# Feed-forward matmuls taken two by two: both products with the weights' high parts, then both with their low parts

## The chip, the cores and the metric

The kernel runs on one core of one Trainium2 chip. The metric is device time in microseconds (us) of one execution; shorter is better. Three executions of the kernel before gave 979.96, 982.59 and 986.15 us; their median is 982.59 us.

## The reference: what is computed

Two layers act on 256 tokens of width 1024. Each layer is a feed-forward block, a mixing block (two kinds of attention, a gated product over tokens, a pooling) and a second feed-forward block, each with a residual:

```python
def swiglu_ffn(x, g, w1, w3, w2):
    h = rms_norm(x, g)
    return (jax.nn.silu(h @ w1) * (h @ w3)) @ w2
...
        x = x + FFN_RES_WEIGHT * swiglu_ffn(x, ffn1_norm[l], ffn1_w1[l], ffn1_w3[l], ffn1_w2[l])
...
        x = x + FFN_RES_WEIGHT * swiglu_ffn(x, ffn2_norm[l], ffn2_w1[l], ffn2_w3[l], ffn2_w2[l])
```

`w1` and `w3` are 1024 x 2816, `w2` is 2816 x 1024, all in float32. So there are four feed-forward blocks in one execution; they are called block 1 to block 4 here.

## The kernel before

**Numbers in two parts.** Every float32 operand of a large product is split into a high part (`h`, or the first half of a tile `hl`), which ScalarE rounds to the type float32r, and a low part (`lo`, or the second half of `hl`), which VectorE gets as the difference (`split`, lines 122 and 123, for weights; `split_scaled` for activations). A product of two such operands is taken as high*high + high*low + low*high.

**The helper `mm2` (lines 149 and 150)** does one such product of a 128x128 block of weights with a 128x256 block of activations. Its first matmul has the weights' high part as the stationary operand and streams 512 columns past it: the activations' high part (256 columns) and low part (256 columns), which lie side by side in one tile. The results go to the two halves of one PSUM bank. Its second matmul has the weights' low part as the stationary operand, streams the 256 columns of the activations' high part, and adds to the first half of the same bank. Every matmul has a weight load of its own, so a product is load, 512 columns, load, 256 columns. The helper `mm3` (lines 143 to 145) serves the mixing block and is untouched; it takes three matmuls of equal width for a product.

**Up stage.** For each of the 22 blocks `m` of 128 hidden units, `up(m)` has one 1 MB tile of weights loaded and split, takes two banks (`j` = 0 for `w1`, 1 for `w3`), and for each of the 8 blocks `k` of the width calls `up_products(m, k)`, which calls `mm2` once for each `j`. That is 16 products for each `m`, 352 for a stage. `act(m)` then adds the halves of each bank (ScalarE line 303, VectorE line 304), applies the norm's factor, SiLU and the gate, and splits the result into `hid[m]` (lines 134 and 135). In block 1, `up_first` takes `m` = 0 and 1 together, piece by piece as their weights land. `rows` and `sums` put a few small matmuls (lines 224 and 243) among the products of `m` = 2 or so.

**Down stage.** `down(c)`, for 8 output blocks `c`, adds up 22 products (one for each `m`, one `mm2` each) in one bank: 176 products for a stage. `finish` adds the result to the residual `x` (line 234).

**What sets the order.** SyncE issues the weight loads, as far ahead as the four raw tiles allow; ScalarE and VectorE split them into four tiles for the two parts. The order on each engine's queue is fixed before the run by the framework's planner, which follows the order of the program but moves ahead of an instruction whose input it expects to be late another one whose inputs it expects to be there. In part of the mixing block the order written is pinned; in the feed-forward blocks it is not. Each engine runs its queue in order.

Of the kernel before, what the change touches and what calls it, by code (L numbers as in the profile page):

```python
# [29 lines left out]
T = 256  # L30
D = 1024
DFF = 2816
NM = DFF // 128
# [37 lines left out]
def tile_macaron(ctx, tc, xT, g0, const0, consts, params, w13, w2, wA, wB, wD, wC, wE, wcmp, wo, out):  # L71
    nc = tc.nc
# [14 lines left out]
    def bank_a():  # L87
        a = banks.tile([128, 512], F32, name="a", tag="bank")
        return a

    def bank_h():
        h = banks.tile([128, 512], F32, name="h", tag="bank")
        return h

    def s2():
        s = tiles.tile([128, 512], F32, name="s", tag="tile")
        return s

    def halves(s):
        return s.rearrange("p (a n) -> p a n", a=2)  # L100
# [11 lines left out]
    def split(src, n, cuts=2, loads=1):  # L112

        h = spl.tile([128, 2048], F32R)
        lo = spl.tile([128, 2048], F32R)
        r = raws.tile([128, 2048], F32)

        def part(a, b):
            nc.sync.dma_start(r[:, a:b], src[:, a:b])
            for i in range(a, b, n // cuts):  # L120
                c = slice(i, min(i + n // cuts, b))
                nc.scalar.activation(h[:, c], r[:, c], AF.Copy)  # L122
                nc.vector.tensor_tensor(lo[:, c], r[:, c], h[:, c].bitcast(F32), op=ALU.subtract)  # L123

        for i in range(loads):
            part(n * i // loads, n * (i + 1) // loads)
        return (h[:, :n], lo[:, :n]) if loads else (h[:, :n], lo[:, :n], part)

    def split_scaled(src, scale, n=T):

        hl = tiles.tile([128, 2 * n], F32R, name="hl", tag="tile")
        th, tl = hl[:, :n], hl[:, n:]
        if scale is None:
            nc.scalar.activation(th, src, AF.Copy)  # L134
            nc.vector.tensor_tensor(tl, src, th.bitcast(F32), op=ALU.subtract)  # L135
        else:
            nc.scalar.activation(th, src, AF.Copy, scale=scale)
            nc.vector.scalar_tensor_tensor(tl, src, scale, th.bitcast(F32), op0=ALU.mult, op1=ALU.subtract)  # L138
        return th, tl, hl
# [4 lines left out]
        nc.tensor.matmul(o, wgt[0], mov[1], start=False, stop=False)  # L144
        return nc.tensor.matmul(o, wgt[1], mov[0], start=False, stop=stop)  # L145

    def mm2(o, wgt, mov, start, stop):

        nc.tensor.matmul(o, wgt[0], mov[2], start=start, stop=False)  # L149
        return nc.tensor.matmul(o[:, :T], wgt[1], mov[0], start=False, stop=stop)  # L150

    g0t = const.tile([128, 8 * L], F32)
    x = const.tile([128, 8, T], F32)
# [77 lines left out]
    def finish(k, accs, factor, norm):  # L231

        for acc in accs:
            nc.vector.scalar_tensor_tensor(x[:, k, :], acc, factor, x[:, k, :], op0=ALU.mult, op1=ALU.add)  # L234
        if norm is not None:
            norm.chunk(k)
        else:
            nc.sync.dma_start(out[:, k, :], x[:, k, :])

    def bcast_rows(rstd):  # L240
        p = bank_h()
        for t in range(2):
            nc.tensor.transpose(p[:, 128 * t:128 * t + 128], rstd[:, t:t + 1].to_broadcast([128, 128]), ident)  # L243
        rb = wk.tile([128, T], F32)
        nc.vector.tensor_copy(rb, p[:, :T])
        return rb

    def ffn(l, f, norm, gain, at_step):

        first = norm is None  # L250
        if first:
            norm = Norm(g0t)
        w13s, hid, w2s, st = {}, {}, {}, {}

        def up_products(m, k):
            h, lo = w13s[m]
            for j in range(2):
                c = slice(256 * k + 128 * j, 256 * k + 128 * j + 128)
                ins = mm2(st[m][j], (h[:, c], lo[:, c]), norm.xs[k], k == 0, k == 7)
            return ins  # L260

        def up_first():

            parts = []
            for m in range(2):
                st[m] = [bank_h(), bank_h()]
                h, lo, part = split(w13[l, f, m], 2048, loads=0)
                w13s[m] = h, lo
                parts.append(part)
            for a, b in ((0, 1), (1, 2), (2, 4), (4, 6), (6, 8)):  # L270
                if a:
                    nc.sync.dma_start(x[:, a:b, :], xT[:, a:b, :])
                if not a:
                    norm.operand(0)
                for part in parts:
                    part(256 * a, 256 * b)
                for k in range(a, b):
                    if k:
                        norm.operand(k)
                for k in range(a, b):  # L280
                    for m in range(2):
                        up_products(m, k)
            for fn in at_step.get(1, ()):
                fn()
            for k in range(8):
                norm.square(k)
            norm.total()

        def up(m, mid={}):
            w13s[m] = split(w13[l, f, m], 2048, cuts=4 if m < 3 else 2, loads=2 if first and m == 2 else 1)  # L290
            for fn in at_step.get(m, ()):
                fn()
            st[m] = [bank_h(), bank_h()]
            for k in range(8):
                ins = up_products(m, k)
                if k in mid:
                    with tc.issue_after(ins.ins):
                        mid[k]()

        def act(m):  # L300
            hr = halves(s2())
            for j in range(2):
                nc.scalar.activation(hr[:, j, :], st[m][j][:, T:], AF.Copy)  # L303
                nc.vector.tensor_tensor(hr[:, j, :], st[m][j][:, :T], hr[:, j, :], op=ALU.add)  # L304
            nc.vector.tensor_tensor(hr, hr, st["rb"].unsqueeze(1).to_broadcast([128, 2, T]), op=ALU.mult)  # L305
            gt = hr[:, 0, :]
            nc.scalar.activation(gt, gt, AF.Silu)  # L307
            nc.vector.tensor_tensor(gt, gt, hr[:, 1, :], op=ALU.mult)  # L308
            hid[m] = split_scaled(gt, None)

        def w2_slot(i):
            w2s[i] = split(w2[l, f, i], 2048, cuts=2)

        def down(c):
            acc = bank_a()
            for m in range(NM):
                i, o = divmod(NM * c + m, 16)
                if i not in w2s:
                    w2_slot(i)
                s = slice(128 * o, 128 * o + 128)  # L320
                mm2(acc, (w2s[i][0][:, s], w2s[i][1][:, s]), hid[m], m == 0, m == NM - 1)
            return halves(acc)

        def sums():
            st["rstd"] = norm.rstd()

        def rows():
            st["rb"] = bcast_rows(st["rstd"])
            act(0)
            act(1)  # L330

        for m in range(NM):
            if not (first and m < 2):
                up(m, ({5: sums, 7: rows} if first else {3: rows}) if m == 2 else {})
            elif m == 0:
                up_first()
            if m == 1 and not first:
                norm.total()
                sums()
            if m > 1:  # L340
                act(m)
        nxt = None if gain is None else Norm(gain)
        for c in range(8):
            acc = down(c)
            finish(c, (acc[:, 0, :], acc[:, 1, :]), 0.5, nxt)
        return nxt
# [608 lines left out]
    norm = None  # L955
    for l in range(L):
# [5 lines left out]
        o, w = _PAR["mix_g"]  # L962
        norm = ffn(l, 0, norm, par[:, o:o + w], steps)
        norm = mixer(l, norm, par)
        norm = ffn(l, 1, norm, None if l == L - 1 else g0t[:, 8 * l + 8:8 * l + 16], {})
# [112 lines left out]
```

## Time and profile before

| | |
|---|---|
| median of three executions | 982.59 us |
| the profiled execution | 982.34 us |
| its span, first to last instruction | 980.5 us |
| TensorE matmul busy | 964.3 us (98%), 5840 matmuls |
| weight loads busy | 838.0 us (85%), 5840 loads |
| VectorE busy | 698.6 us (71%) |
| ScalarE busy | 530.6 us (54%) |
| mean granted TensorE clock | 0.996 of full speed |

Times are in us from the start of the span. PE is TensorE's matmuls, PEld its weight loads, which run beside the matmuls; DVE is VectorE, ACT ScalarE. L149 is line 149 of the kernel. The duration shown for a matmul reaches from its start to a modelled end, and successive matmuls overlap: two rows with 0.40 and 0.28 us start again after some 0.35 us. What a matmul costs TensorE in a dense stretch is therefore read from one start to the next start, not from its duration.

### The profile page before, as it was taken

What the parts mean: (1) busy time and instruction counts of PE and PEld (TensorE: products, weight loads), DVE (VectorE), ACT (ScalarE), POOL (GpSimd) and SP (SyncE); (2) the same over time, 40 slices, a digit from 0 to 9 for tenths busy, and PEclk for the clock granted to TensorE, in tenths of its full rate; (3) what the DMA queues carried; (4) which work ended last, traced back from release to release, by engine and by line L of the source; (5) the groups of instructions that cost most, each with busy time, mean ns of one, the idle gap of its engine ahead of it and who ended that gap; (6) DMA issues with size and microseconds to landing.
All of it is one profiled execution on the core that took longest, in us unless ns stands there. A gap on an engine that the chain in (4) does not pass through costs nothing. (4 is left out here: it accounts for less than half of the span.)

```text
span 980.5 us, 14915 instructions
## 1 busy us (share of the span) xinstructions
PE 964.3 (98%) x5840; PEld 838.0 (85%) x5840; DVE 698.6 (71%) x1256; ACT 530.6 (54%) x971; POOL 66.0 (7%) x67
## 2 busy tenths in 40 slices
PE   8999999999989999999999999999998999999998
PEld 6888888898869888888888888889987898888887
DVE  5987776575778777776667777755666787777751
ACT  7655555363566555655445655544545665555530
POOL 2000000031102000000010000001220030000000
PEclk9999999999999999999999999999999999999999
DMA  8965554445426655555555555545453455555530
GB/s 306 338 230 196 172 191 174 159 145 215 173 94 233 232 173 189 197 172 196 191 172 187 200 172 188 197 152 184 169 203 114 150 211 175 177 196 188 177 108 17
DMA packets 28150, 179.28 MB, mean 183 GB/s; under 512 B 3248, under 2 KB 5168, under 8 KB 8240
## 3 DMA queue, kind: packets, MB, share of 16 engines
q1 hardware_dynamic: 27792, 178.19, 52.1%
q8 instruction: 46, 0.75, 0.3%
q10 hardware_dynamic: 288, 0.14, 0.1%
q14 instruction: 24, 0.20, 0.1%
HBM read 177.27 MB, written 1.05 MB: 182 GB/s over the span
## 5 line engine op out<-in xcount | busy, mean ns | idle before, releaser
L123 DVE TENSOR_TENSOR lo<-r,h 128x1024 fp32r<-128x1024 f32 (+4 forms) x346 | 391.7, 1148 | 163.4 <-ACT h L122 162.7
L149 PE MATMUL h<-hl,h 128*128 128x512 f32 x1408 | 498.7, 399 | 1.4 <-ACT h L122 0.8
L122 ACT ACTIVATE h<-r 128x1024 fp32r<-128x1024 f32 (+4 forms) x346 | 327.8, 973 | 268.1 <-issue 230.6
L150 PE MATMUL h<-hl,lo 128*128 128x256 f32 x1408 | 395.3, 281 | 0.5 <-DVE lo L123 0.5
L149 PEld LDWEIGHTS h<-hl,h 128*128 128x128 f32 x1408 | 264.4, 188 | 67.9 <-DVE hl L138 1.5
L150 PEld LDWEIGHTS h<-hl,lo 128*128 128x128 f32 x1408 | 265.8, 189 | 2.1 <-DVE lo L123 2.1
L149 PE MATMUL a<-hl,h 128*128 128x512 f32 x704 | 246.9, 395 | 0.0
L150 PE MATMUL a<-hl,lo 128*128 128x256 f32 x704 | 197.3, 280 | 0.0
L149 PEld LDWEIGHTS a<-hl,h 128*128 128x128 f32 x704 | 131.9, 187 | 31.5 <-DVE hl L135 0.9
L150 PEld LDWEIGHTS a<-hl,lo 128*128 128x128 f32 x704 | 133.0, 189 | 0.0
L234 DVE SCALAR_TENSOR_TENSOR x<-a,x 128x256 f32<-128x256 f32 x80 | 32.9, 421 | 49.0 <-PE a L150 45.3
L304 DVE TENSOR_TENSOR s<-h,s 128x256 f32<-128x256 f32 x176 | 65.9, 415 | 1.1 <-ACT s L303 1.1
L305 DVE TENSOR_TENSOR s<-s,rb 128x512 f32<-128x512 f32 x88 | 60.9, 692 | 2.8
L134 ACT ACTIVATE hl<-s 128x256 fp32r<-128x256 f32 x92 | 38.2, 417 | 43.4 <-DVE s L308 33.9
L303 ACT ACTIVATE s<-h 128x256 f32<-128x256 f32 x176 | 56.5, 371 | 2.7 <-PE h L150 2.7
L211 POOL TENSOR_TENSOR s<-s 128x512 f32<-128x512 f32 x12 | 16.8, 1402 | 593.3 <-ACT s L207 593.3
L143 PE MATMUL a<-h,hl 128*128 128x384 f32 (+2 forms) x128 | 45.8, 358 | 0.0
L307 ACT ACTIVATE s<-s 128x256 f32<-128x256 f32 x88 | 35.5, 404 | 17.9 <-DVE s L305 17.8
L145 PE MATMUL a<-h,hl 128*128 128x384 f32 (+2 forms) x128 | 45.0, 351 | 0.0
L144 PE MATMUL a<-lo,hl 128*128 128x384 f32 (+2 forms) x128 | 44.9, 351 | 0.0
L135 DVE TENSOR_TENSOR hl<-s,hl 128x256 fp32r<-128x256 f32 x92 | 38.4, 419 | 3.4 <-ACT hl L134 3.4
L308 DVE TENSOR_TENSOR s<-s 128x256 f32<-128x256 f32 x88 | 36.8, 419 | 3.4 <-ACT s L307 3.4
(187 smaller groups left out, 779.1 us busy)
## 6 DMA issues: line engine op xcount, KB each, us to landing
r<-in_w_dram SPq DMA_DIRECT2D x129, 1024.0 KB, 4.8
r<-in_wcmp_dram SPq DMA_DIRECT2D x8, 1024.0 KB, 4.8
r<-in_wo_dram SPq DMA_DIRECT2D x8, 1024.0 KB, 5.4
r<-in_wE_dram SPq DMA_DIRECT2D x4, 1024.0 KB, 4.7
r<-in_wC_dram SPq DMA_DIRECT2D x4, 1024.0 KB, 4.7
r<-in_wD_dram SPq DMA_DIRECT2D x4, 800.0 KB, 4.3
r<-in_wA_dram SPq DMA_DIRECT2D x4, 768.0 KB, 4.4
r<-in_wB_dram SPq DMA_DIRECT2D x4, 768.0 KB, 4.3
```

Source lines behind the costliest of these rows:

```text
L122: nc.scalar.activation(h[:, c], r[:, c], AF.Copy)
L123: nc.vector.tensor_tensor(lo[:, c], r[:, c], h[:, c].bitcast(F32), op=ALU.subtract)
L134: nc.scalar.activation(th, src, AF.Copy)
L135: nc.vector.tensor_tensor(tl, src, th.bitcast(F32), op=ALU.subtract)
L143: nc.tensor.matmul(o, wgt[0], mov[0], start=start, stop=False)
L144: nc.tensor.matmul(o, wgt[0], mov[1], start=False, stop=False)
L145: return nc.tensor.matmul(o, wgt[1], mov[0], start=False, stop=stop)
L149: nc.tensor.matmul(o, wgt[0], mov[2], start=start, stop=False)
L150: return nc.tensor.matmul(o[:, :T], wgt[1], mov[0], start=False, stop=stop)
L303: nc.scalar.activation(hr[:, j, :], st[m][j][:, T:], AF.Copy)
L304: nc.vector.tensor_tensor(hr[:, j, :], st[m][j][:, :T], hr[:, j, :], op=ALU.add)
L305: nc.vector.tensor_tensor(hr, hr, st["rb"].unsqueeze(1).to_broadcast([128, 2, T]), op=ALU.mult)
```

## The change

`mm2` goes, and `mm2x2` takes its place. It is given two products and issues four matmuls: the 512 columns of the first product, the 512 columns of the second, the 256 columns of the first, the 256 columns of the second. In the up stage the two products are `j` = 0 and 1 of one `k`: they have the same activations and two different banks. In the down stage they are `m` and `m + 1` of one `c`, with different activations and the same bank. `NM` is 22 and a weight tile of the down stage holds 16 blocks, so both products of a pair always lie in one tile. The number of matmuls and of weight loads, their widths and the data that they read are as before, and so is everything outside `up_products` and `down`.

```diff
-    def mm2(o, wgt, mov, start, stop):
-
-        nc.tensor.matmul(o, wgt[0], mov[2], start=start, stop=False)
-        return nc.tensor.matmul(o[:, :T], wgt[1], mov[0], start=False, stop=stop)
+    def mm2x2(os, wgts, movs, starts, stops):
+
+
+        for o, wgt, mov, start in zip(os, wgts, movs, starts):
+            nc.tensor.matmul(o, wgt[0], mov[2], start=start, stop=False)
+        for o, wgt, mov, stop in zip(os, wgts, movs, stops):
+            ins = nc.tensor.matmul(o[:, :T], wgt[1], mov[0], start=False, stop=stop)
+        return ins
...
             h, lo = w13s[m]
-            for j in range(2):
-                c = slice(256 * k + 128 * j, 256 * k + 128 * j + 128)
-                ins = mm2(st[m][j], (h[:, c], lo[:, c]), norm.xs[k], k == 0, k == 7)
-            return ins
+            c = [slice(256 * k + 128 * j, 256 * k + 128 * j + 128) for j in range(2)]
+            return mm2x2(st[m], [(h[:, s], lo[:, s]) for s in c], (norm.xs[k],) * 2, (k == 0,) * 2, (k == 7,) * 2)
...
-            for m in range(NM):
+            for m in range(0, NM, 2):
                 i, o = divmod(NM * c + m, 16)
                 if i not in w2s:
                     w2_slot(i)
-                s = slice(128 * o, 128 * o + 128)
-                mm2(acc, (w2s[i][0][:, s], w2s[i][1][:, s]), hid[m], m == 0, m == NM - 1)
+                w = [(w2s[i][0][:, s], w2s[i][1][:, s]) for s in (slice(128 * o, 128 * o + 128),
+                                                                  slice(128 * o + 128, 128 * o + 256))]
+                mm2x2((acc, acc), w, (hid[m], hid[m + 1]), (m == 0, False), (False, m == NM - 2))
```

## Rows read from the trace of the kernel before

**Rows 1.** The page's first part: busy time, share of the span and instructions of each engine.

```profile
PE 964.3 (98%) x5840; PEld 838.0 (85%) x5840; DVE 698.6 (71%) x1256; ACT 530.6 (54%) x971; POOL 66.0 (7%) x67
```

**Rows 2.** The page's costliest groups, those of the two lines that the change touches: h is a bank of the up stage, a one of the down stage. Columns: count, busy us, mean ns of one, idle us of the engine just before them and what ended it.

```profile
L149 PE MATMUL h<-hl,h 128*128 128x512 f32 x1408 | 498.7, 399 | 1.4 <-ACT h L122 0.8
L150 PE MATMUL h<-hl,lo 128*128 128x256 f32 x1408 | 395.3, 281 | 0.5 <-DVE lo L123 0.5
...
L149 PE MATMUL a<-hl,h 128*128 128x512 f32 x704 | 246.9, 395 | 0.0
L150 PE MATMUL a<-hl,lo 128*128 128x256 f32 x704 | 197.3, 280 | 0.0
```

**Rows 3.** Two stretches of the table by windows, the load-paced beginning and a stretch in block 2: length, busy us (count) of PE, PEld, DVE, ACT and POOL, granted clock, mean busy share of the DMA engines, GB/s.

```profile
0.00:50.00 50.00, 46.58 (x240) 38.01 (x241) 38.27 (x62) 33.26 (x59) 7.95 (x13) 1.00 0.90 321
...
300.00:400.00 100.00, 100.00 (x587) 87.59 (x586) 79.04 (x127) 60.17 (x107) 7.93 (x5) 1.00 0.57 200
```

**Rows 4.** The timeline of PE in the up stage of block 2: start us, duration us, instruction. The last row is the start of the product 30 products after the first one.

```profile
330.30 0.40 PE L149 MATMUL h<-hl,h 128*128 128x512 f32 x1
330.54 0.28 PE L150 MATMUL h<-hl,lo 128*128 128x256 f32 x1
330.66 0.40 PE L149 MATMUL h<-hl,h 128*128 128x512 f32 x1
330.89 0.28 PE L150 MATMUL h<-hl,lo 128*128 128x256 f32 x1
331.01 0.40 PE L149 MATMUL h<-hl,h 128*128 128x512 f32 x1
...
340.90 0.40 PE L149 MATMUL h<-hl,h 128*128 128x512 f32 x1
```

**Rows 5.** The timeline of PE in the down stage of block 1; the last row again 30 products after the first.

```profile
160.25 0.39 PE L149 MATMUL a<-hl,h 128*128 128x512 f32 x1
160.48 0.28 PE L150 MATMUL a<-hl,lo 128*128 128x256 f32 x1
160.60 0.39 PE L149 MATMUL a<-hl,h 128*128 128x512 f32 x1
...
170.65 0.39 PE L149 MATMUL a<-hl,h 128*128 128x512 f32 x1
```

**Rows 6.** The timeline of PE in the mixing block of layer 1, where `mm3` issues only matmuls of 256 columns, all into one half of a bank, each with a load of other weights: first and last of 31 in a row, 30 steps.

```profile
205.31 0.28 PE L145 MATMUL h<-hl,lo 128*128 128x256 f32 x1
...
208.90 0.28 PE L145 MATMUL h<-hl,lo 128*128 128x256 f32 x1
```

**Rows 7.** The same where `mm3` issues only matmuls of 512 columns, three in a row into the same bank: first and last of 29 in a row, 28 steps.

```profile
224.51 0.39 PE L144 MATMUL a<-lo,hl 128*128 128x512 f32 x1
...
230.86 0.40 PE L145 MATMUL a<-h,hl 128*128 128x512 f32 x1
```

**Rows 8.** The timeline of PE where the dense feed-forward work begins and ends: block 1 from 33.79 on (what lies before is paced by loads) to the mixing block's first matmul; block 2, which runs into block 3 at 492.47 without a break; the first matmul after block 3; first and last product of block 4.

```profile
33.79 0.40 PE L149 MATMUL h<-hl,h 128*128 128x512 f32 x1
...
196.31 0.34 PE L143 MATMUL a<-h,hl 128*128 128x384 f32 x1
...
305.98 0.40 PE L149 MATMUL h<-hl,h 128*128 128x512 f32 x1
...
492.47 0.39 PE L149 MATMUL h<-hl,h 128*128 128x512 f32 x1
...
680.09 0.34 PE L143 MATMUL a<-h,hl 128*128 128x384 f32 x1
...
789.91 0.40 PE L149 MATMUL h<-hl,h 128*128 128x512 f32 x1
...
976.06 0.39 PE L149 MATMUL a<-hl,h 128*128 128x512 f32 x1
```

**Rows 9.** The table by windows for line 149 alone, dense part of block 1: length, PE busy us (count; one of them began before the window), clock, DMA share, GB/s.

```profile
33.78:196.30 162.52, 162.50 (x463) 1.00 0.58 200
```

**Rows 10.** The timeline of PE in block 4 around the small matmuls of the norm; two products lie between the first pair of rows and two between the second pair.

```profile
800.86 0.40 PE L149 MATMUL h<-hl,h 128*128 128x512 f32 x1
...
802.01 0.40 PE L149 MATMUL h<-hl,h 128*128 128x512 f32 x1
...
804.13 0.40 PE L149 MATMUL h<-hl,h 128*128 128x512 f32 x1
...
805.05 0.40 PE L149 MATMUL h<-hl,h 128*128 128x512 f32 x1
```

**Rows 11.** The waits of the weight loads on these lines over the whole span: tile, line, released by, us in total, times, longest us.

```profile
PEld h L150 <- DVE lo L123: 2.1, 5, 0.5
...
PEld a L149 <- DVE hl L135: 0.9, 4, 0.2
```

**Rows 12.** The timeline of all engines at the wait of block 1's down stage: the last `act`, the last split of `hid`, the weight load that waited for it (idle us before it, and its releaser, in brackets).

```profile
143.63 0.64 ACT L303 ACTIVATE s<-h 128x256 f32<-128x256 f32 x2
...
144.32 0.42 DVE L135 TENSOR_TENSOR hl<-s,hl 128x256 fp32r<-128x256 f32 x1
...
144.79 0.19 PEld L149 LDWEIGHTS a<-hl,h 128*128 128x128 f32 x1 [0.22 <-DVE hl L135]
```

**Rows 13.** The timeline in the up stage of block 1: a matmul of 256 columns, the weight load that runs beside it, and the matmul that needs those weights.

```profile
100.45 0.28 PE L150 MATMUL h<-hl,lo 128*128 128x256 f32 x1
100.45 0.19 PEld L149 LDWEIGHTS h<-hl,h 128*128 128x128 f32 x1
100.57 0.40 PE L149 MATMUL h<-hl,h 128*128 128x512 f32 x1
```

## The prediction, written before the changed kernel ran

> **What bounds the kernel now.** First the page's shares: TensorE is busy 98% of the span, VectorE 71%, ScalarE 54% [rows 1]. Then the costliest groups: nearly all of that is the two lines of the change, 2112 products of a 512-column and a 256-column matmul, with under 2 us of idle time before them [rows 2]. Then the table by windows, to see whether anything else comes close: after the beginning, where the DMA engines are 0.90 busy, VectorE has 79 of 100 us, the DMA engines 0.57, and the granted clock is 1.00, full speed, 2.4 GHz [rows 3]. So the feed-forward blocks end when TensorE has pushed its columns through, and only the step from one matmul's start to the next matters.
>
> So I read these steps, from the timeline, and they hold the case. In the up stage 30 products take 340.90 - 330.30 = 10.60 us, 353.3 ns each, and a single one among them takes 0.36 us [rows 4]. In the down stage of block 1 the same 30 products take 10.40 us, 346.7 ns each [rows 5]: same widths, same loads, same clock. Where only one width is issued, 256 columns cost (208.90 - 205.31)/30 = 119.7 ns [rows 6] and 512 columns (230.86 - 224.51)/28 = 226.8 ns [rows 7]. Their sum is 346.5 ns, the quick product of rows 5. So alternating widths has two gaits, one at the price of the separate widths and one about 6.7 ns dearer, and it stays in one for many products.
>
> **How much is in the dear gait.** Against 346.67 ns for each product [rows 5]:
> - block 1 from 33.79: 196.31 - 33.79 = 162.52 us for 462 products [rows 8, 9], 160.16 at that price: 2.36 over;
> - block 2: 186.49 us for 528 (22 x 16 + 8 x 22), 183.04: 3.45 over;
> - block 3: 187.62 us for 528: 4.58 over;
> - block 4: 186.15 us for 527, 182.70: 3.45 over [rows 8].
>
> Together 13.84 us. Not all is gait: the norm's small matmuls make two stretches of two products 1.15 and 0.92 us long where 0.69 would do, 0.69 us in all [rows 10], in blocks 2 to 4 (in block 1 they lie before 33.79); and in each down stage one load waits for the last `hid`, 0.9 us over the four [rows 11]. 13.84 - 3 x 0.69 - 0.9 = **10.9 us** for the dear gait, over 2045 products.
>
> **The change part by part.** It removes no matmul and no load and moves no DMA. Per pair of products it replaces 512, 256, 512, 256 by 512, 512, 256, 256: one step 512 to 512 and one 256 to 256 come in; of the four changes of width two go.
>
> *The new steps.* 512 to 512 with other weights and the same bank is measured, 226.8 ns, and 256 to 256, 119.7 ns [rows 6, 7]. That excludes a penalty for two sums into one bank in a row, which is what the down stage now does.
>
> *The changes of width that stay*, one each way in every pair, have no row in this surrounding. Bounds: the two together cost what they do in the quick gait (346.7) or in the dear one (353.3) [rows 4, 5]. At the first the pair costs 693.3 and all 10.9 us go; at the second half of it stays, 5.5 us are gained. I take the first: half the neighbours are now of the kind that stays at its plain price through a whole stretch, and the quick gait shows that a change of width need cost nothing. The second is a rival.
>
> *A rule against it.* The rows say that equal widths run at 346.5 ns for a pair of one each, and alternating ones at 346.7 or 353.3 [rows 4 to 7]. The Trainium skill, page "TensorE: Matmul & The Clock Gate", section "Back-to-back issue gap", gives the isolated gap as columns over 2.4 GHz plus some 2.5 ns, a function of the width alone. By that rule order is worth nothing and the sum stays at 982.3 us. The trace agrees with it only where the quick gait holds, and its steps of 119.7 and 226.8 ns are some 13 ns, not 2.5, above the columns' time.
>
> *Waiting for the weights' low part.* It is needed one 512-column step later. In the beginning five loads waited for it, 2.1 us [rows 11]; each can gain at most one step of 0.227, 1.1 us in all, and nothing if the next load is then late. I take 0.
>
> *The first accumulator of an up block* ends later: its last matmul is now followed by 120 ns of TensorE's work, where it was followed by a whole product, so ScalarE can begin `act` some 0.23 us later. What hides it: `act` of the last block ran at 143.63, nine us after that stage's products (they end near 134.8), so it was waiting behind other work on ScalarE's queue [rows 12]. If that cover went, 0.23 us for each stage, 0.9 in all.
>
> *The pair with `hid[21]`* asks for it one matmul (0.227) before the low part of product 20, instead of after it (0.12 more). The load already waits 0.22 us for that result [rows 12]. Between 0 and 0.35 us in each of four stages, 0 to 1.4; the wait stands some 10 us, 28 products, after the stage's start near 134.8, though `hid[21]` belongs to the 22nd, so the planner had put products of the next output block ahead of it; and what ends the wait is VectorE's time, not TensorE's order, so I take 0.
>
> *What comes next if TensorE gets 2% quicker:* VectorE at 79% and DMA at 0.57 [rows 3] both have room; loads and splits follow the buffers that TensorE frees. The mixing block and the tail are unchanged.
>
> **Sum.** 982.34 (the profiled execution, 0.25 under the median) - 10.9 = 971.4, and with the median's 0.25 about **971.6 us**, 1.1% less.
>
> **The rivals.**
> - *Half stays (976.9 us).* The dear gait sits in the change of width itself and is paid once per pair, not twice. For it: only alternating stretches show it. Against: the quick gait alternates too.
> - *Order is worth nothing (982.3 us).* Either the two gaits are set by something other than the change of width, say by how a stretch was entered, and the new order falls into a dear one as often; the rule of width alone gives this too. Or the planner, which places matmuls by itself, undoes the pairing. For it: block 1's gait differs between stages with the same instructions [rows 4, 5]. Against: no stretch of equal widths is dear.
> - *Slower (998.7 us at full price).* Two 256-column matmuls in a row leave two loads in a row with only 120 ns of cover each; a load is 0.19 us long and starts with the matmul that it runs beside, 0.12 before the matmul that needs it [rows 13]. If the second comes late, each product may cost the long step of 0.36 us [rows 4]: 13.3 ns over the quick one, x 2045 = 27.3 us, less the 10.9 paid now, +16.4. It decides from the point where a pair costs over 706.7 ns; 1% slower needs about 9.5 ns more. Against: 256-column steps with loads of other weights hold 119.7 ns [rows 6].
>
> **How the numbers follow.** All of the dear gait goes: 0.47. Half stays: 0.26. Nothing: 0.15. Slower: 0.12. The three executions before lie 6 us apart, 0.6%, so each case is some 3 us wide. Faster or slower by 1%, about what a measurement of this kernel can tell, means below 972.8 or above 992.4. The first case lies only 1.2 us inside, so two thirds of it count as faster, 0.30, and 0.02 of the second; most of the slower case's chance and a little of planning mishap give 0.10 above; the rest, 0.58, is no change by that measure. The range reaches from the first case less the 1.1 us of earlier waits and 2 us of scatter, 968.5, to the third with its scatter, 984.0; the likeliest case's own range is 968.5 to 974.5.
>
> **What would show it.** In the changed profile's timeline a pair should take 0.69 us, from one first 512-column start to the next such start, through whole stages: 30 products in 10.40 us in the up stages as in the down stages. 10.50 would be the half case, 10.60 the third, more the fourth. The blocks should be shorter by about 2.1, 2.5, 3.7 and 2.5 us (the sums above less the odd steps), the mixing stretches unchanged, and the row of waits for `hid` should stay at 0.9 us. It would be wrong if the two changes of width left in a pair cost more than 347 ns together, or if products stood in the old order.

## The result, and the profile after

The changed kernel takes **974.74 us** (973.53 to 975.51, five executions) against 982.85 us before (979.96 to 986.15, five executions, the three above among them): ratio 0.9904, 95% interval 0.9885 to 0.9923. That is 8.1 us less, inside the range given, between the forecast of 971.6 and the rival "half stays" at 976.9, and within 1%. The profiled execution took 975.51 us, span 973.7 us, 6.8 us under the span before. Among the runs below stand three single executions of 3952 to 5351 us; the ratios leave them out, and they move a median by 0.4 us at most.

The page's first part, and its groups for the two lines that took the place of lines 149 and 150 (columns as in [rows 1, 2]):

```profile
PE 958.2 (98%) x5840; PEld 834.9 (86%) x5840; DVE 697.6 (72%) x1256; ACT 531.0 (55%) x971; POOL 68.0 (7%) x67
...
L151 PE MATMUL h<-hl,h 128*128 128x512 f32 x1408 | 443.5, 396 | 0.8 <-DVE hl L138 0.5
...
L153 PE MATMUL h<-hl,lo 128*128 128x256 f32 x1408 | 277.1, 278 | 0.3 <-DVE lo L123 0.3
L151 PE MATMUL a<-hl,h 128*128 128x512 f32 x704 | 221.9, 396 | 0.0
...
L153 PE MATMUL a<-hl,lo 128*128 128x256 f32 x704 | 138.7, 278 | 0.0
```

The shares say little: TensorE is as busy as before, 98%. The busy time of line 151 (443.5 after 498.7 us) is no saving of 55 us: neighbours of one group now overlap, and what overlaps is counted once. The steps have to be read again. The timeline of PE in the up stage of block 2, where [rows 4] stood before; the last row begins 15 pairs, 30 products, after the first:

```profile
330.25 0.63 PE L151 MATMUL h<-hl,h 128*128 128x512 f32 x2
330.72 0.40 PE L153 MATMUL h<-hl,lo 128*128 128x256 f32 x2
330.95 0.63 PE L151 MATMUL h<-hl,h 128*128 128x512 f32 x2
331.42 0.39 PE L153 MATMUL h<-hl,lo 128*128 128x256 f32 x2
...
340.70 0.63 PE L151 MATMUL h<-hl,h 128*128 128x512 f32 x2
```

10.45 us for 30 products: 696.7 ns a pair, 348.3 a product. It was 353.3 [rows 4] or 346.7 [rows 5]. The same sum holds in every dense stretch of every stage, up and down; the two gaits are gone, and one between them has come.

The timeline of PE at the first product, at the 67th (where [rows 8] begin, at 33.79 before), then where the blocks begin and end:

```profile
6.26 1.04 PE L151 MATMUL h<-hl,h 128*128 128x512 f32 x2 [0.46 <-DVE hl L138]
...
33.07 0.62 PE L151 MATMUL h<-hl,h 128*128 128x512 f32 x2
...
194.33 0.34 PE L143 MATMUL a<-h,hl 128*128 128x384 f32 x1
...
305.17 0.63 PE L151 MATMUL h<-hl,h 128*128 128x512 f32 x2
...
490.11 0.63 PE L151 MATMUL h<-hl,h 128*128 128x512 f32 x2
...
675.03 0.34 PE L143 MATMUL a<-h,hl 128*128 128x384 f32 x1
...
784.65 0.63 PE L151 MATMUL h<-hl,h 128*128 128x512 f32 x2
```

| stretch | before, us | after, us | difference | forecast |
|---|---|---|---|---|
| block 1, first 66 products (from 6.22 before) | 27.57 | 26.81 | -0.76 | 0 |
| block 1, dense rest | 162.52 | 161.26 | -1.26 | -2.1 |
| mixing block 1 | 109.67 | 110.84 | +1.17 | 0 |
| block 2 | 186.49 | 184.94 | -1.55 | -2.5 |
| block 3 | 187.62 | 184.92 | -2.70 | -3.7 |
| mixing block 2 | 109.82 | 109.62 | -0.20 | 0 |
| block 4, to the end of the span | 190.59 | 189.05 | -1.54 | -2.5 |

With 0.04 us at the start this adds up to the 6.8 us. The feed-forward blocks gave 7.8 us, of which 7.1 lie in their dense parts; 1.2 were lost in a mixing block that the change does not touch (the last section shows where). The 0.76 us at the beginning of block 1, where loads set the pace, cannot be put down to the change: in the three profiles of the changed kernel that beginning takes 26.4, 26.8 and 28.4 us. That the whole of block 1 came out near its forecast is luck.

The waits of the weight loads, as in [rows 11]; they hardly moved:

```profile
PEld h L153 <- DVE lo L123: 2.0, 4, 0.7
...
PEld h L151 <- DVE hl L138: 1.2, 1, 1.2
...
PEld a L151 <- DVE hl L135: 1.2, 4, 0.3
```

### The profile page after: what moved, and what is told of

Its sections match the earlier page's. It is cut to its first block, busy times and chain, and to the rows that moved or that the text cites. A ratio compares the mean times of both kernels' runs of the same rounds, so it can differ in the third digit from the quotient of the medians.

```text
span 973.7 us, 14899 instructions
## 1 busy us (share of the span) xinstructions
PE 958.2 (98%) x5840; PEld 834.9 (86%) x5840; DVE 697.6 (72%) x1256; ACT 531.0 (55%) x971; POOL 68.0 (7%) x67
## 5 line engine op out<-in xcount | busy, mean ns | idle before, releaser
L151 PE MATMUL h<-hl,h 128*128 128x512 f32 x1408 | 443.5, 396 | 0.8 <-DVE hl L138 0.5
L153 PE MATMUL h<-hl,lo 128*128 128x256 f32 x1408 | 277.1, 278 | 0.3 <-DVE lo L123 0.3
L151 PE MATMUL a<-hl,h 128*128 128x512 f32 x704 | 221.9, 396 | 0.0
L151 PEld LDWEIGHTS h<-hl,h 128*128 128x128 f32 x1408 | 214.6, 189 | 1.9 <-DVE hl L138 1.2
L153 PE MATMUL a<-hl,lo 128*128 128x256 f32 x704 | 138.7, 278 | 0.0
L151 PEld LDWEIGHTS a<-hl,h 128*128 128x128 f32 x704 | 107.5, 189 | 1.3 <-DVE hl L135 1.2
L143 PE MATMUL a<-hl,h 128*128 128x256 f32 x128 | 39.3, 307 | 0.1
```

What stands on the lines that cost most here:

```text
L143: nc.tensor.matmul(o, wgt[0], mov[0], start=start, stop=False)
L153: ins = nc.tensor.matmul(o[:, :T], wgt[1], mov[0], start=False, stop=stop)
```

## The experiments

Times are medians; each ratio is to executions of the kernel before on the same chip. The theory put to the test: TensorE's price for a product depends on the order of widths and on what ran just before, and on nothing else of the kernel.

### Matmuls alone, in fourteen orders

After loading and splitting two weight tiles, only matmuls run, 64 products a stretch (`N = 64`; `hi` is 512 columns with the high part, `low` 256 with the low):

```diff
+        for p in range(0, N, 4):
+            for q in range(p, p + 4):
+                hi(H, q)
+            for q in range(p, p + 4):
+                low(W, q)
```

> Leaves out the whole computation but the loads and splits of two weight tiles and of x; after that only matmuls run, in stretches of 64 products each (512 columns with the high part, then 256 with the low part, in different orders and widths), each order twice. Theory 1, the change of width costs: alternating (g1) 346.7 or 353.3 ns a product, pairs (g2, and g2s with one bank) 348.3, groups of four (g4) about 347.5, of eight and more 346.7 to 347; snake (512, 256, 256, 512) as g2; other (512 and 256 into different banks) as g1. Theory 2, it is the sum into the same bank directly after: other at 346.7 although it alternates, g2s dearer than g2. Theory 3, it is the neighbours (ScalarE, VectorE and DMA traffic of the full kernel): every order at 346.7. Theory 4, the weight load has too little cover beside 256 columns: with 384 or 320 columns in place of 256 (a384, a320) the step sum is the plain one (columns/2.4 + 13.3 ns each: 400.0 and 373.3), with 128 (a128) it is far above the plain 293.3; theory 1 has a384 and a320 above the plain sum too.

From the starts in the timeline, whole cycles only (without the first alternating stretch, which still waited for loads); "plain" is what [rows 5 to 7] give, columns/2.4 + 13.3 ns a matmul:

| order | ns a product (or a pair of widths) | plain |
|---|---|---|
| alternating, banks by turns | 346.7 | 346.7 |
| alternating, 512 and 256 in different banks | 353.4 | 346.7 |
| pairs, two banks / one bank | 348.3 / 348.3 | 346.7 |
| 512, 256, 256, 512 | 348.4 | 346.7 |
| groups of 4 / 8 / 16 | 350.8 / 349.1 / 347.9 | 346.7 |
| 512 with 384 / 320 / 128, alternating | 413.3 / 379.9 / 340.2 | 400.0 / 373.3 / 293.3 |
| 384 with 256 / 384 with 384 | 293.4 / 347.1 | 293.3 / 346.7 |

The groups of four in the timeline of this kernel, 12 groups from the first row to the last but one; line 1032 is 512 columns, line 1035 is 256:

```profile
397.60 1.09 PE L1032 MATMUL h<-hl,h 128*128 128x512 f32 x4
398.53 0.64 PE L1035 MATMUL h<-hl,lo 128*128 128x256 f32 x4
...
414.44 1.09 PE L1032 MATMUL h<-hl,h 128*128 128x512 f32 x4
415.37 0.64 PE L1035 MATMUL h<-hl,lo 128*128 128x256 f32 x4
```

(414.44 - 397.60)/48 = 350.8 ns a product. Three theories fall. Both gaits and the price of the pairs appear with VectorE, ScalarE and the DMA queues at rest (no instruction of either engine and a DMA share of 0.00 from 36 to 320 us), so the surroundings are not their cause. One bank or two makes no difference to pairs. Little cover for a load is not it either: with 384 columns, where a load has more cover, the excess is 13.3 ns, larger than with 256. Nor does "fewer changes cost less" hold as it stood: groups of four are dearer than pairs. The excess per cycle is 3.3 ns for pairs, 17 for fours, 20 for eights and sixteens. In the long groups it sits in the first five or so 512s after a 256, whose steps are 233, 236, 228, 232, 231 ns where 226.7 is plain; the first 256, at 113 ns, gives a part back. In pairs both 512s take 233 ns, and the 256-column steps, at 115 and 116 ns, give most of it back. Groups of 64, which have no second cycle in a stretch, show the same five steps.

That alternating ran quick here with one bank scheme and dear with another left bank and entry mixed up, so they were crossed.

### The same order after different entries

```diff
+    def entry(kind):
+        for i in range(8):
+            nc.tensor.matmul(lone[:, :kind], w[0][0][:, 128 * i:128 * i + 128], xs[i][2][:, :kind], start=True, stop=True)
...
+    entry(384)
+    emit(mm_two_384_h, mm_two_384_l, two, 256, alt)
```

> Leaves out the whole computation but the loads and splits of two weight tiles and of x. Stretches of 32 alternating products (512, 256), each entered after eight matmuls of 256, 512, 384 or 128 columns or after a wait on VectorE, with the two banks by turns (two), one bank for all (one), or 512 and 256 in different banks (other); also pairs after two of the entries, and 448 and 192 columns in place of 256. Theory A, the entry sets the gait: the same entry gives the same gait with every bank scheme, and different entries differ. Theory B, the banks set it: two and one at 346.7 ns a product after every entry, other at 353.3 after every entry. Pairs stay at 348.3 after both entries in both theories. Plain sums for 448 and 192 columns would be 426.7 and 320.0 ns.

Alternating products ran at 346.7 ns after the 384-column entry in six stretches of six, with all three bank schemes; after 128 columns and after a wait on VectorE at 353.3 in twelve of twelve; after 256 and after 512 columns at 353.3 in ten of twelve. The same bank scheme after two entries, 30 products from the second row of each pair to the third (lines 1009 and 1015 are the 512-column matmuls after the entry with 384 and with 128):

```profile
282.24 0.39 PE L1009 MATMUL h<-hl,h 128*128 128x512 f32 x1
...
282.59 0.39 PE L1009 MATMUL h<-hl,h 128*128 128x512 f32 x1
...
292.99 0.39 PE L1009 MATMUL h<-hl,h 128*128 128x512 f32 x1
...
294.18 0.45 PE L1015 MATMUL h<-hl,h 128*128 128x512 f32 x1
...
294.58 0.40 PE L1015 MATMUL h<-hl,h 128*128 128x512 f32 x1
...
305.18 0.40 PE L1015 MATMUL h<-hl,h 128*128 128x512 f32 x1
```

10.40 and 10.60 us, the two numbers of [rows 5] and [rows 4]. In these stretches the entry sets the gait (theory A), though after 256 or 512 columns it can fall either way (one of the two exceptions began while the granted clock was still 0.50), and each gait then lasts to the stretch's end. Pairs ran at 348.3 after both of their entries. 448 and 192 columns in place of 256 gave 437.8 and 340.0 ns, 11.1 and 20.0 over the plain sums.

### One stage at a time

`up_only` keeps the old `down`; `down_only` and `down_only2` (the same kernel) keep the old `up_products`:

```diff
-            for m in range(0, NM, 2):
+            for m in range(NM):
...
-                mm2x2((acc, acc), w, (hid[m], hid[m + 1]), (m == 0, False), (False, m == NM - 2))
+                mm2(acc, (w2s[i][0][:, s], w2s[i][1][:, s]), hid[m], m == 0, m == NM - 1)
```

> The up stage in pairs, the down stage as before. If the gain is that of the dear gait, nearly all of it is in the up stages, which were dear all through: 974.5 to 976, that is 7 to 8 us under the kernel before. If the pairing of the down stage gives its share by number of products (a third), 977 to 978.

> The down stage in pairs, the up stage as before. Theory of the gaits: three of four down stages ran at 346.7 ns a product already and a pair costs 696.7, so 0.15 us are lost in each of those and about 0.9 gained in the dear one: 982 to 983, no change. If pairing gains on every product alike: 980.

> The down stage alone in pairs, once more: it came out 6 us faster where at most 3.2 us were expected (0.8 for each of four stages, if all four had been dear). On this chip, if the gaits are all there is, 980 to 982 beside 982 (ratio 0.997 to 1.000); if pairing the down stage has another effect, 0.994 again.

`up_only`: 976.46 beside 986.31 us, 0.9902 (0.9872 to 0.9933). `down_only`: 979.73 beside the same, 0.9939 (0.9914 to 0.9964), more than was expected of the gaits; on another chip `down_only2` gave 980.15 beside 980.88, 0.9995 (0.9975 to 1.0015), as expected. The first was not repeated on its chip, where the kernel before took 984 to 988 us; the last section has a reason why such executions differ, but that it was the cause there is not shown.

Both profiles of this kernel hold something that the theory does not foresee. In block 1's up stage TensorE has the same matmuls in the same order as in the kernel before, back to the start of the program; yet 30 products there take 10.40 us (the rows are from `down_only`) and not 10.60 as in both profiles of the kernel before:

```profile
90.18 0.40 PE L158 MATMUL h<-hl,h 128*128 128x512 f32 x1
...
100.58 0.40 PE L158 MATMUL h<-hl,h 128*128 128x512 f32 x1
```

Over the stage's 286 dense products that is 1.9 us, which the pairs in the down stage did not bring directly. So the order of the matmuls before a stretch does not fix its gait by itself; what else does, and whether every execution of this kernel runs so, is not shown. The up stages of blocks 2 to 4 were dear in both. The up stage of block 2, first product to the down stage's first, in `up_only` and then in `down_only2`:

```profile
303.41 0.63 PE L151 MATMUL h<-hl,h 128*128 128x512 f32 x2
...
426.72 0.40 PE L158 MATMUL a<-hl,h 128*128 128x512 f32 x1
```
```profile
303.26 0.40 PE L158 MATMUL h<-hl,h 128*128 128x512 f32 x1
...
428.28 0.64 PE L151 MATMUL a<-hl,h 128*128 128x512 f32 x2
```

123.31 against 125.02 us: in blocks 2 to 4 the gain lies in the up stages.

### Both kernels again

> The kernel before, once more, with a profile on this chip: ratio 1.00. It shows which gait its stages take on another execution: up stages at 353.3 ns a product as before in both theories; the down stages at 346.7 or 353.3, which decides whether pairing the down stage alone can gain (0.8 us for each dear one) or not.

> The changed kernel, once more, beside the others on the same chip: pairs at 696.7 ns in all stages of every execution (348.3 a product), ratio 0.990. If pairs too had two gaits, some stage would show another step sum.

> The changed kernel once more, on the same chip as the run before it: ratio 0.990 to 0.993, stages at 348.3 ns a product.

The kernel before came out at 0.9985 (0.9958 to 1.0011), and its down stages were dear in blocks 1 and 3 (62.3 us from first to last matmul) and mostly quick in 2 and 4 (61.4): the gait differs between executions of one program. The changed kernel came out at 974.59 us, 0.9934 (0.9909 to 0.9959), and 976.02 us, 0.9919 (0.9892 to 0.9946), with down stages of 61.3 to 61.5 us and up stages of blocks 2 to 4 of 123.2 to 123.4 us in both profiles: no second gait.

### Larger groups in the kernel

`up4` takes two `k` together in the up stage, `all16` all eight, and eleven `m` in the down stage:

```diff
-            for k in range(8):
-                ins = up_products(m, k)
+            ins = up_all(m)
+            for k in range(8):
                 if k in mid:
```

> The up stage in groups of four (four times 512 columns, then four times 256; the first two blocks of block 1 stay in pairs), the down stage in pairs. Theory that fewer changes of width cost less: 347.5 ns a product at most, 1 us under the changed kernel or the same. The stretch of matmuls alone measured 350.8 ns a product for groups of four against 348.3 for pairs: if that price holds in the kernel, 1376 products x 2.5 = 3.4 us over the changed kernel.

> Groups of 16 in the up stage (all 16 products of an m with the high parts, then all with the low parts; the first two blocks of block 1 in pairs) and of 11 in the down stage. From the stretches of matmuls alone a change from 256 to 512 columns costs about 20 ns once 512s follow for long, whatever the group's size: 347.9 ns a product for 16 and 346.67 + 20/11 = 348.5 for 11. So the up stages gain 0.4 x 1376 = 0.6 us and the down stages lose 0.1: 0.5 us under the changed kernel, not to be told from it. If fewer changes cost in proportion less (1.67 a product for a change in every two), 347.0: 2.6 us under it. Slower would mean that a wait took its place (the low parts of all blocks are asked for together, weight tiles of the down stage are held longer).

`up4`: 977.47 beside 982.11 us, 0.9960 (0.9932 to 0.9987), 2.9 us over the changed kernel on that chip (3.4 expected); the up stages of blocks 2 and 4 are 124.01 us long, against 123.21. The price of the bare matmuls carries over.

`all16`: 976.59 beside 980.88 us, 0.9954 (0.9935 to 0.9972). Its up stages in blocks 2 to 4 are 123.05 to 123.07 us long, 0.15 under the 123.2 of pairs, as expected. In block 1 the norm's small matmuls, hung on a `k`, wait longer for GpSimd. The row of waits in the changed kernel and in `all16`, then the table by windows for PE from 6 to 34 us in `all16` and in `after_third`, the changed kernel once more (length, busy us, count, granted clock, DMA share, GB/s):

```profile
PEld h L247 <- POOL rs L232: 0.7, 1, 0.7
PEld h L247 <- POOL rs L232: 1.7, 1, 1.7
```
```profile
6.00:34.00 28.00, 25.71 (x135) 0.94 0.98 357
6.00:34.00 28.00, 25.66 (x134) 0.94 0.93 333
```

The other two profiles of the changed kernel have 143 and 146 matmuls in this window, at clock 1.00. But the third lost as much here without the larger group, so that the group costs more than the 1.0 us of wait is not shown. The gain in steps is too small to be told in time, and the changed kernel did not run on this chip.

### Steering the old order

If the entry sets the gait, a few matmuls of 384 columns should pull the old order into the quick one. `steer` adds four, `steer_one` one, into a bank that nobody reads; `steer_one` has the down stage in pairs.

```diff
+            if m == 3 or (m == 0 and not first):
+                steer(w13s[m][0])
...
+        def steer(h):
+            e = bank_h()
+            nc.tensor.matmul(e[:, :384], h[:, :128], norm.xs[0][2][:, :384], start=True, stop=True)
```

> The kernel before (alternating 512 and 256) with four more matmuls of 384 columns, into a bank that nobody reads, ahead of the products of m = 0 (blocks 2 to 4) and of m = 3 (all blocks): 28 matmuls, 28 x 0.173 = 4.8 us of added work. Theory, the gait is set by what ran just before: the up stages go at 346.7 ns a product from m = 3 on, 20 instead of 26 gaits' worth of dear products: 66 x 16 + 19 x 16 = 1360 products x 6.67 = 9.1 us less, so 4 us faster than the kernel before in spite of the added work, down stages perhaps quick at their start too. Rival, the surroundings of the full kernel pull it back to 353.3: 4.8 us slower. If waits within the stage flip it, something between, seen in the timeline as the place where 10.40 us for 30 products turns into 10.60.

> Up stage alternating as before, but with one matmul of 384 columns (into a bank that nobody reads) ahead of m = 0 (blocks 2 to 4) and of m = 3: 7 x 0.173 = 1.2 us added. Down stage in pairs, 348.3 ns a product. If one such matmul puts the up stage into the quick gait as four did: 1360 products at 346.7, 1.67 under pairs, 2.3 us less and 1.2 more: about 1 us under the changed kernel, too little to be told from it in time, but to be seen in the stages' rows (about 122.8 us from first to last product in blocks 2 to 4, against 123.2). If one is not enough: up stages at 353.3, 124.9 us long, and the time 5 to 6 us above the changed kernel.

The timeline of PE in `steer`, block 2: the four matmuls (line 265), the first product, and later 30 products of the up stage (from the third row to the last):

```profile
304.57 0.86 PE L265 MATMUL h<-hl,h 128*128 128x384 f32 x4
305.27 0.39 PE L149 MATMUL h<-hl,h 128*128 128x512 f32 x1
...
335.15 0.39 PE L149 MATMUL h<-hl,h 128*128 128x512 f32 x1
...
345.55 0.39 PE L149 MATMUL h<-hl,h 128*128 128x512 f32 x1
```

10.40 us: code that was dear in all four up stages before now runs quick in all four, but for the products between the norm's small matmuls and the next 384s. Block 1 proves nothing, since it ran quick in `down_only` without any steering; blocks 2 to 4 do, since without added matmuls the old order was dear there in all twelve stages profiled. The time was 981.45 beside 980.88 us, 1.0013 (0.9993 to 1.0033): no change that can be told, with some 4.8 us of added work. The 4 us of gain that I expected did not come. By the rows the up stages of blocks 2 and 4 gave 0.84 us each, the added matmuls counted, about what was expected of them. But the down stages of blocks 2 to 4 began at 346.6 ns a product and ran at 353.3 from the wait for the last `hid` on; they were dear at 62.1 to 62.2 us, where the profile before has one such stage. That took back some 1.4 us; where the rest went is not shown. At the same wait three of the four down stages before had turned from 353.3 to 346.7, so it can go either way. `steer_one`, in block 2, from its one added matmul to the first down product:

```profile
306.94 0.34 PE L273 MATMUL h<-hl,h 128*128 128x384 f32 x1
307.12 0.40 PE L158 MATMUL h<-hl,h 128*128 128x512 f32 x1
...
430.00 0.63 PE L151 MATMUL a<-hl,h 128*128 128x512 f32 x2
```

From the added matmul on 123.06 us, for what took 125.02 with the old order alone (`down_only2`) and 123.31 in pairs (`up_only`). Its time is 975.14 beside 984.49 us, 0.9923 (0.9893 to 0.9953), against 976.02 for the changed kernel on the same chip. By the rows it is 0.25 us quicker than pairs in such a stage, about 1 us in all, too little to be told in time: as good as the changed kernel, not shown to be better.

## Why the prediction was right or wrong, point by point

- **What bounds the kernel, and where the gain had to be:** right. The time came from the steps of TensorE in the feed-forward blocks; `up_only` carries it (0.9902); with the down stage alone in pairs `down_only2` shows none that can be told in time (0.9995).
- **The 10.9 us in the dear gait:** right as a sum. `steer` shows that it is no property of the stages: in blocks 2 to 4 four matmuls of another width ahead take it away.
- **"Half the neighbours are now of the kind that stays at its plain price", hence 693.3 ns a pair:** this step failed. A pair costs 696.7 ns, 3.3 more, which over some 1020 pairs makes 3.4 us; the dense parts missed the forecast by 3.8 (7.1 us where 10.9 were forecast), 0.3 of it in the waits for `hid`. The price lies between the bounds given (693.3 and 700.0), a quarter of the dear gait's excess and not none or half. The reasoning was wrong in kind: the neighbours do not have prices that add up. In pairs 512 to 512 takes some 233 ns and not 226.8 [rows 7], 256 to 256 some 115 and not 119.7 [rows 6], and groups of four, with fewer changes still, are dearer. Only the whole cycle's sum can be read.
- **The quick stages of before as a bound:** used for the sum, but not for its loss. Down stages that ran quick went from 61.4 to 61.5 us.
- **Two waits and one delay taken at 0:** right but for 0.3 us. The wait for `lo` hardly moved (2.0 after 2.1 us), that for the last `hid` went from 0.9 to 1.2 us (inside its bounds of 0 to 1.4, not at the 0 taken), and nobody waited for the up stage's accumulators.
- **"Order is worth nothing":** its time did not come, and the rule of width alone that stood beside it falls for these matmuls. But one reason given for it, that the gait is set by how a stretch was entered, is what `m2_entries` and `steer` show. Pairs escaped it: they ran at one price after both entries tried and in every stage of three profiles. The Trainium skill, "TensorE: Matmul & The Clock Gate", section "Back-to-back issue gap", gives a gap by width and no price of order; the runs have 346.7, 348.3, 350.8 and 353.3 ns for the same two widths.
- **"Slower", two loads in a row with too little cover:** did not come. Something like it shows with narrower matmuls: 512 with 192 and 512 with 128 columns both cost 340 ns, where the plain sums are 320.0 and 293.3, so going from 192 to 128 columns saved nothing. That the loads set this floor is not shown. The Trainium skill, "TensorE: Matmul & The Clock Gate", section "LDWEIGHTS (loading the stationary operand)", gives columns over 1.2 GHz, by which a load of 128 would take an estimated 107 ns; no run here times a load alone, and the trace's rows have 0.19 us for one beside a matmul [rows 13].
- **Chances:** "no change by 1%" had 0.58 and came. The profiled execution alone would have given 0.7%; mixing block 1 took 1.2 us of it, and the beginning of block 1 gave 0.76 that nobody had forecast. The time lay in the range, but the most likely case, all of the dear gait gone, is not the one that came.

What makes the two gaits inside TensorE, what besides the entry decides between them, and why a pair settles at 3.3 ns over the plain sum, stays open.

## What to carry to other kernels

In a dense stretch read TensorE from start to start over whole cycles: a few ns a product, times two thousand, were what there was to win here. Two matmul widths with other weights each time can run in more than one lasting rhythm, so try a few orders with bare matmuls, all in one run, and take the price of the whole cycle; the sum of separate steps misled, and groups of four were worse than pairs. What is hung on such a group at its seams has to be looked at again as well.

## What the runs showed that was not expected

**The scatter between executions goes largely with the granted clock, which falls in the mixing blocks.** Beside `steer` the kernel before took 978.0 and 978.5 us where the mean granted clock was 0.998, and 983.4 and 986.0 where it was 0.992 and 0.991. The table by windows for PE in mixing block 1, kernel before and then after (length, busy us, count, clock, DMA share, GB/s):

```profile
265.00:270.00 5.00, 4.85 (x44) 1.00 0.02 3
270.00:275.00 5.00, 2.50 (x14) 0.75 0.21 29
275.00:280.00 5.00, 5.00 (x41) 0.91 0.44 182
```
```profile
265.00:270.00 5.00, 2.88 (x25) 0.98 0.00 0
270.00:275.00 5.00, 4.49 (x21) 0.50 0.55 184
275.00:280.00 5.00, 5.00 (x39) 0.84 0.07 28
```

In both executions TensorE had no matmul for 2.6 us (269.85 to 272.50 before, 267.88 to 270.51 after, waiting for ScalarE), and by the end of that gap the granted clock stood at its lower level, 1.2 GHz. In the execution after it stayed there through the whole of 270 to 275, where 4.49 us of matmuls ran at half speed, and in the one before for about half of that window. That is where the 1.2 us of mixing block 1 lie, and differences of this kind are as large as what was being measured. Every profile of a whole kernel has such a stretch in each mixing block, and two have one in the beginning of block 1.

**One matmul of another width, 0.17 us of useless work, shortens the up stages of blocks 2 to 4 by some 2 us each.** A kernel whose price depends on what ran before can change its time by an edit elsewhere.
